# Four of a quad's seven products in one PSUM bank, and two more pairs with two quad chunks

## The chip, the cores and the metric

The kernel runs on one NeuronCore of one Trainium2 chip. The metric is the device time of one execution in microseconds; lower is better. A time is given as the median of several runs, and one further execution is recorded by the hardware profiler: its rows are what the text below reads.

## The reference, cut to what matters

One decoder layer over 256 tokens of width 2048: a mixer of three branches (differential attention, a convolution module, chunkwise retention) with gates, a cross-attention into 256 memory tokens, and a SwiGLU feed-forward network, each behind an RMS norm.

```python
proj = h @ w_in                         # 2048 -> 15360 columns
...
merged = g0 * (ya @ w_branch[0]) + g1 * (yb @ w_branch[1]) + g2 * (yr @ w_branch[2])
x = x + merged @ w_out
...
q = h @ wq; k, v = split(m @ wkv)       # cross-attention
x = x + o @ wo
...
a, b = split(h @ w13)                   # 2048 -> 2 x 5632
x = x + (silu(a) * b) @ w2              # 5632 -> 2048
```

Everything is float32, and nearly all of the work is the products with the weights, 449.63 MB of HBM reads in all.

## The kernel before

The token axis is two tiles of 128 (t = 0, 1). A weight matrix is read in chunks of 512 rows by 512 columns; a half of one (256 rows, two k-slices of 128) is a tile `raw` of 128 x 1024. Each half is split into a high part `wh` (fp32r, a cast on ScalarE, `hi_of`) and a low part `wl` (a subtract on VectorE, `lo_of`). TensorE then multiplies three times for each k-slice: activation high by weight high, high by low, low by high, each 128 x 128 by 128 x 512 columns (`products`, L293). So a half against both token tiles is 12 matmuls.

`pair` (L405) makes two blocks of 512 output columns, W0 and W1, from four activation chunks. An "N" chunk has four halves (two for each block), 48 matmuls. An "S" chunk uses seven products instead of eight (a quad, `quad_jobs`, L332), each of 6 matmuls, 42 in all. Weight tiles of such products are sums of quarters: `add` (VectorE) puts one tile onto another, and `gd(..., accum_op=ALU.add)` lets a DMA on GpSimd's queue add one from HBM. The tile t["a"] goes b11, +b12, +b22, +b21 in place and serves p1, p5, p6 and p4 in turn; t["b"] serves p7. The activation side has four combinations made once by `factors`. `MODES2` is SSNN, `MODES1` is SNNN, `MODES0` is NNNN; there are 26 pairs of this kind, in the input projection, the memory's key and value projection, the output projections, and the feed-forward network.

PSUM has eight banks. The pool `psm` holds two buffers of two banks (tiles `mm`), one for each block: ps0 and ps1, where [0] and [1] are the two token tiles. The pool `pst` has four single banks (tiles `tp`). In the kernel before, p1, p5, p6 and p7 of both S chunks are each added up in a `tp` bank of their own, and read out: join1 (a ScalarE copy of 512), join5, join6 and join7 (one, two and two VectorE steps of 512) collect them into two SBUF tiles x0 and x1. p2 and p4 go to ps0's two banks, p3 to ps1's first, on top of the N halves. `done` adds x to the finished buffer (one VectorE add of 1024 for each block) and hands it to the pair's evacuation function. The order of the code is p1, p2 and p5, p3 and p6 mixed with block 0's N halves, then p7, p4 mixed with block 1's first N halves, done for block 0, the rest of block 1, done for block 1.

The order on each engine is not the code's: the tile framework orders instructions by a simulated timeline, with waits put in where tiles and banks need them. DMAs keep the code's order on their queues. `emit_unit` prepares four units ahead (LA = 4), so a unit's cast and subtract are called for before the matmuls of the unit four places earlier. `hlp` has five buffers each for wh and wl, `rawp` ten for raw.

Of the kernel before, what the change touches and what calls it, by code (L numbers as in the profile page):

```python
# [13 lines left out]
ALU = mybir.AluOpType  # L14
# [43 lines left out]
def trunk(ctx, tc, xT, xtok, memT, memtok, w_in, w_br, w_out, w_q, w_kv, w_o, w_13, w_2,  # L58
          prm, cst, decay, gfin, out):
    nc = tc.nc  # L60
    P = 128
# [11 lines left out]
    pin = [False]  # L73
# [19 lines left out]
    def gd(**kw):  # L93
        tc.keep_in_program_order(nc.gpsimd.dma_start(**kw))  # L94
# [10 lines left out]
    def S4(shape, dt=F32):  # L105
        return s4.tile(shape, dt, tag="s4", name=nm("s4"))
# [67 lines left out]
    def call(fn):  # L174
        items.append(("call", fn))
# [117 lines left out]
    def products(u, only=None, final=True):  # L293
        a = u["act"]
        for k in range(2):
            for ps, key, k0, t, kind in u["prods"]:
                if only is not None and t not in only:
                    continue
                ah, al = lhs(a, kind, (t, k0) if kind == "n" else t, k)
                o = ps[key]  # L300
                fl = (id(ps), key)
                pe.matmul(o, ah, u["hi"][:, k, :], start=fl in u["start"] and k == 0, stop=False)
                pe.matmul(o, ah, u["lo"][:, k, :], start=False, stop=False)
                pe.matmul(o, al, u["hi"][:, k, :], start=False, stop=fl in u["stop"] and k == 1)
# [27 lines left out]
    def quad_jobs(pp, ps0, ps1, w0, w1, a):  # L332
# [62 lines left out]
        def f4(u):  # L395
            parts(u, t.pop("a"))

        return dict(p1=unit(pp, 1, 0, 0, "n", f1, b11=w0[:, 0:2, :]),
                    p2=unit(ps0, 0, 2, 0, "n", f2, b21=b21, b12=w1[:, 0:2, :]), p5=unit(pp, 5, 0, 0, "s", f5),
                    p3=unit(ps1, 0, 0, 3, "s", f3, b22=b22), p6=unit(pp, 6, 0, 1, "s", f6),  # L400
                    p7=unit(pp, 7, 0, 2, "s", f7), p4=unit(ps0, 1, 2, 1, "n", f4))

    insb = [False]

    def pair(W0, W1, acts, modes, evac0, evac1):  # L405


        ps0, ps1, pp = {}, {}, {}
        xs = []
        us = []  # L410
        sset = [c for c in range(len(acts)) if modes[c] == "S"]
        nset = [c for c in range(len(acts)) if modes[c] == "N"]

        def enter():
            settle(3)
            cap[0] = 3
            pin[0] = True

        def join1():
            x0, x1 = S4([P, 2, 512]), S4([P, 2, 512])  # L420
            xs.extend([x0, x1])
            sc.copy(x0[:, 0, :], pp.pop(1))

        def join5():
            ve.tensor_tensor(out=xs[1][:, 1, :], in0=pp.pop(5), in1=xs[0][:, 0, :], op=ALU.add)

        def join6():

            p = pp.pop(6)
            ve.tensor_tensor(out=xs[1][:, 0, :], in0=p, in1=xs[1][:, 1, :], op=ALU.subtract)  # L430
            ve.tensor_tensor(out=xs[0][:, 1, :], in0=p, in1=xs[0][:, 0, :], op=ALU.subtract)

        def join7():
            p = pp.pop(7)
            ve.tensor_tensor(out=xs[0][:, 1, :], in0=p, in1=xs[0][:, 1, :], op=ALU.subtract)
            ve.tensor_tensor(out=xs[1][:, 1, :], in0=xs[1][:, 0, :], in1=p, op=ALU.subtract)
            cap[0] = 4

        def done(n, ps, evac):
            def f():  # L440
                x = xs[n]
                ve.tensor_tensor(out=x, in0=ps["m"], in1=x, op=ALU.add)
                xs[n] = None
                insb[0] = True
                evac(x)
                insb[0] = False
            return f

        call(enter)
        quads = [quad_jobs(pp, ps0, ps1, W0[c], W1[c], acts[c]) for c in sset]  # L450
        n0, n1 = (each_half(ps, [W[c] for c in nset], [acts[c] for c in nset]) for ps, W in ((ps0, W0), (ps1, W1)))

        def units_of(*names):
            return [q[n] for m in names for q in quads for n in m]

        first = units_of(("p1",), ("p2", "p5"), ("p3", "p6"))
        marks = {len(quads) - 1: join1, 3 * len(quads) - 1: join5, 5 * len(quads) - 1: join6}

        def marked(i, f):
            def g():  # L460
                u = f()
                if i in marks:
                    call(marks[i])
                return u
            return g

        us += mixed([marked(i, f) for i, f in enumerate(first)], n0)
        us += [f() for f in units_of(("p7",))]
        call(join7)
# [1110 lines left out]
```

## Time and profile before

| what | us |
|---|---|
| median of three runs (1997.3, 2001.64, 2002.55) | 2001.64 |
| the profiled execution's own time | 1998.88 |
| its span | 1997.1 |
| PE, DVE and ACT busy | 1979.9, 1666.9, 1120.4 |

In the profile PE is TensorE, DVE VectorE, ACT ScalarE, POOL GpSimd, and SP the engine whose queue loads the weights. PEld is TensorE's weight load, which runs beside the matmuls. Nearly every instruction goes through one helper and has the line L86, so instructions are told apart by their tiles: `wh`, `wl` and `raw` as above, `mm` and `tp` the two kinds of PSUM tiles, `s` the SBUF work tiles. Matmuls are pipelined and their ends are modelled; a distance between starts is a better price than a length. A table by stretches gives the busy time of each engine in a window of the span; a row of the timeline ends with the idle time before it and who ended it.

### The profile page before, as it was taken

Reading aid. Unit: us, or ns where it says so; the run is one execution under the profiler, and the core shown is the slowest. Engines: PE = TensorE matmul, PEld = TensorE weight load, DVE = VectorE, ACT = ScalarE, POOL = GpSimd, SP = SyncE. Lnnn points to the kernel's source line nnn. Section 1 sums busy time; section 2 is a strip of 40 time slices with the busy share of each in tenths; the row PEclk is TensorE's granted clock in tenths of the full one; section 3 lists DMA queues with packets and bytes.
Section 4 is the critical chain, followed back from the end, with each engine's and each line's share of the span. In section 5 each row is a group of like instructions: output and inputs, shape, how many; then the busy total and the mean of one; then the engine's idle time right before and its main releaser. Section 6 shows DMA issues by size and latency. Waiting matters only on the chain.

```text
span 1997.1 us, 25285 instructions
## 1 busy us (share of the span) xinstructions
PE 1979.9 (99%) x9081; PEld 1636.8 (82%) x9081; DVE 1666.9 (83%) x2040; ACT 1120.4 (56%) x1343; POOL 129.8 (6%) x172
## 2 busy tenths in 40 slices
PE   9999999999999999999999999999999999999998
PEld 7888888888788887888888888888888878878886
DVE  6997689778887788989988565899988999889974
ACT  7444343548655556655566554665655665655653
POOL 0000000000100001000111000000001000011000
PEclk9999999999999999999999999999999999999999
DMA  9656555554777788689898544957888978988891
GB/s 377 206 193 197 180 177 166 180 170 151 214 208 240 235 262 257 221 263 283 274 295 304 191 158 136 287 177 224 271 274 276 275 231 252 301 278 260 256 329 61
DMA packets 128285, 463.88 MB, mean 232 GB/s; under 512 B 14368, under 2 KB 14624, under 8 KB 128160
## 3 DMA queue, kind: packets, MB, share of 16 engines
q1 hardware_dynamic: 105552, 380.46, 54.1%
q0 software_dynamic: 22464, 81.80, 19.3%
q8 instruction: 71, 1.16, 0.2%
q14 instruction: 54, 0.44, 0.1%
q10 hardware_dynamic: 144, 0.01, 0.0%
HBM read 449.63 MB, written 12.58 MB: 231 GB/s over the span
## 4 chain that ended last, share of the span: by engine, by line
PE 79%; issue 9%; DVE 6%; DMA 4%; POOL 1%; ACT 1%; SPq 0%; ACTq 0%; POOLq 0%; DVEq 0%
PE mm L86 64%; PE tp L86 15%; DVE wl L86 3%; DVE s L86 2%; DMA raw<-in_w 2%; DMA raw<-in_w_kv 1%; DMA raw<-in_w_in 1%; POOL raw L94 1%; DVE raw L86 1%; ACT wh L86 1%; DMA s<-in_memtok 0%; SPq L97 0%; POOL s L94 0%; ACTq L1575 0%; POOL x2d L94 0%
## 5 line engine op out<-in xcount | busy, mean ns | idle before, releaser
L86 PE MATMUL mm<-wh,s 128*128 128x512 f32 x4568 | 1443.9, 391 | 3.5 <-ACT wh L86 3.3
L86 ACT CAST wh<-raw 128x1024 fp32r<-128x1024 f32 (+1 forms) x855 | 886.4, 1051 | 728.7 <-PE mm L86 474.9
L86 DVE TENSOR_TENSOR wl<-raw,wh 128x1024 fp32r<-128x1024 f32 (+1 forms) x855 | 1020.8, 1217 | 252.7 <-ACT wh L86 241.3
L86 PEld LDWEIGHTS mm<-wh,s 128*128 128x128 f32 x4568 | 857.7, 188 | 183.1 <-ACT wh L86 7.0
L86 PE MATMUL mm<-wl,s 128*128 128x512 f32 x2284 | 893.2, 391 | 4.4 <-DVE wl L86 4.4
L86 PEld LDWEIGHTS mm<-wl,s 128*128 128x128 f32 x2284 | 429.5, 188 | 97.3 <-DVE wl L86 9.3
L86 PE MATMUL tp<-wh,s 128*128 128x512 f32 x864 | 288.5, 392 | 0.0
L86 PEld LDWEIGHTS tp<-wh,s 128*128 128x128 f32 x864 | 162.2, 188 | 33.1
L86 PE MATMUL tp<-wl,s 128*128 128x512 f32 x432 | 168.1, 389 | 0.0
L86 DVE TENSOR_TENSOR s<-s,s 128x1024 f32<-128x1024 f32 (+4 forms) x144 | 140.8, 986 | 1.7 <-ACT wh L86 1.1
L86 DVE TENSOR_TENSOR s<-tp,s 128x512 f32<-128x512 f32 (+1 forms) x166 | 109.6, 683 | 16.4 <-PE tp L86 11.7
L86 DVE TENSOR_TENSOR raw<-raw,raw 128x1024 f32<-128x1024 f32 x100 | 121.0, 1216 | 0.4
L86 DVE SCALAR_TENSOR_TENSOR s<-s,prm_t,s 128x256 fp32r<-128x256 f32 (+25 forms) x256 | 105.8, 461 | 0.0
L86 DVE TENSOR_TENSOR s<-mm,s 128x1024 f32<-128x1024 f32 (+1 forms) x70 | 83.1, 1187 | 20.3 <-PE mm L86 20.1
L86 PEld LDWEIGHTS tp<-wl,s 128*128 128x128 f32 x432 | 81.2, 188 | 16.2
L86 ACT ACTIVATE s<-s 128x512 f32<-128x512 f32 (+1 forms) x60 | 46.2, 771 | 63.3 <-DVE s L86 51.4
L94 POOL DMA_DIRECT2D raw<-in_w x54 | 47.7, 883 | 431.8 <-DVE wl L86 188.4
L86 PE MATMUL tp<-cst_t,s 128*128 128x128 f32 x408 | 57.1, 272 | 0.0
L86 PEld LDWEIGHTS tp<-cst_t,s 128*128 128x128 f32 x408 | 48.6, 140 | 9.0 <-issue 0.3
L86 PE MATMUL tp<-s,s 128*128 128x256 f32 (+4 forms) x348 | 53.5, 314 | 0.0
L86 PEld LDWEIGHTS tp<-s,s 128*128 128x128 f32 (+1 forms) x348 | 46.1, 189 | 5.8 <-issue 0.5
L86 ACT COPY s<-tp 128x512 f32<-128x512 f32 (+1 forms) x69 | 35.8, 528 | 15.0 <-PE tp L86 13.3
(88 smaller groups left out, 503.2 us busy)
## 6 DMA issues: line engine op xcount, KB each, us to landing
raw<-in_w SPq DMA_DIRECT2D x264, 512.0 KB, 6.5
raw<-in_w_in SPq DMA_DIRECT2D x239, 512.0 KB, 4.6
raw<-in_w_kv SPq DMA_DIRECT2D x64, 512.0 KB, 5.4
raw<-in_w POOLq DMA_DIRECT2D x54, 512.0 KB, 8.5
raw<-in_w_br SPq DMA_DIRECT2D x48, 512.0 KB, 6.5
raw<-in_w_out SPq DMA_DIRECT2D x32, 512.0 KB, 7.6
raw<-in_w_q SPq DMA_DIRECT2D x32, 512.0 KB, 5.1
raw<-in_w_o SPq DMA_DIRECT2D x32, 512.0 KB, 4.0
```

Of the source, the lines that this page charges most:

```text
L86: i = f(*a, **k)
L94: tc.keep_in_program_order(nc.gpsimd.dma_start(**kw))
```

## The change

p1, p6, p7 and p4 now share one bank, ps1[1] (in `quad_jobs`, c1 is ps1 and its key 1). The four are added up on top of each other in it; between them ScalarE copies out the running sum: keep1 after p1, keep(0) after p6, keep(1) after p7, and done1's copy at the end. Only p5 still has a `tp` bank. p2 goes to ps1[0], p3 to ps0[0]. VectorE subtracts p5's bank from two of the copies, adds block 0 (1024) in done0, and adds only half of block 1 (512) in done1. The two blocks' roles in the quad are exchanged, and the signs in `factors` follow. p6 comes before p3; f6 now does the add of b22 and starts the accumulating DMA of b21, and b22's raw tile is held from p6 to p3. The last N half of block 0 is put behind p7 instead of ahead of it. In the first pair of the key and value projection and in the feed-forward pair i = 1 MODES1 becomes MODES2.

```diff
-                pe.matmul(o, ah, u["hi"][:, k, :], start=fl in u["start"] and k == 0, stop=False)
+                sk = dict(skip_group_check=True) if ps.get("open") and key == 1 else {}
+                pe.matmul(o, ah, u["hi"][:, k, :], start=fl in u["start"] and k == 0, stop=False, **sk)
...
-        def f3(u):
-            r = raw(ix["b22"])
-            add(t["a"], r)
-            parts(u, r)
-            raws.pop(ix["b22"])
-
         def f6(u):
+            t["r"] = raw(ix["b22"])
+            add(t["a"], t["r"])
             parts(u, t["a"])
             gd(out=t["a"], in_=b21, accum_op=ALU.add)
 
+        def f3(u):
+            parts(u, t.pop("r"))
+            raws.pop(ix["b22"])
...
-        return dict(p1=unit(pp, 1, 0, 0, "n", f1, b11=w0[:, 0:2, :]),
-                    p2=unit(ps0, 0, 2, 0, "n", f2, b21=b21, b12=w1[:, 0:2, :]), p5=unit(pp, 5, 0, 0, "s", f5),
-                    p3=unit(ps1, 0, 0, 3, "s", f3, b22=b22), p6=unit(pp, 6, 0, 1, "s", f6),
-                    p7=unit(pp, 7, 0, 2, "s", f7), p4=unit(ps0, 1, 2, 1, "n", f4))
+        return dict(p1=unit(c1, 1, 0, 0, "n", f1, b11=w0[:, 0:2, :]),
+                    p2=unit(c1, 0, 2, 0, "n", f2, b21=b21, b12=w1[:, 0:2, :]), p5=unit(pp, 5, 0, 0, "s", f5),
+                    p6=unit(c1, 1, 0, 1, "s", f6, b22=b22), p3=unit(c2, 0, 0, 3, "s", f3),
+                    p7=unit(c1, 1, 0, 2, "s", f7), p4=unit(c1, 1, 2, 1, "n", f4))
...
+        def keep1():
+            xs.extend([S4([P, 2, 512]), S4([P, 2, 512])])
+            sc.copy(xs[1][:, 0, :], ps1[1])
+
+        def keep(i):
+            def f():
+                x = xs[0][:, i, :]
+                sc.copy(x, ps1[1])
+                ve.tensor_tensor(out=x, in0=pp[5], in1=x, op=ALU.subtract)
...
+        def done1():
+            x = xs[1]
+            ve.tensor_tensor(out=x[:, 0, :], in0=ps1[0], in1=x[:, 0, :], op=ALU.add)
+            sc.copy(x[:, 1, :], ps1[1])
...
+        us += mixed(units_of(("p1",), then=keep1) + units_of(("p2", "p5"))
+                    + units_of(("p6",), then=keep(0)) + units_of(("p3",)), n0[:-1])
+        us += [f() for f in units_of(("p7",), then=keep(1))]
+        us.append(n0[-1]())
+        call(done0)
         us += mixed(units_of(("p4",)), n1[:len(n1) // 2])
-        call(done(0, ps0, evac0))
         us += [f() for f in n1[len(n1) // 2:]]
-        call(done(1, ps1, evac1))
+        call(done1)
...
-            pair(w0, w1, mm, MODES2 if m or h else MODES1, ev_kv(dst[h]), ev_kv(dst[h + 1]))
+            pair(w0, w1, mm, MODES2, ev_kv(dst[h]), ev_kv(dst[h + 1]))
...
-                pair(w0, w1, x2n, MODES1 if i == 1 else MODES2, ev_a(i), ev_b(i))
+                pair(w0, w1, x2n, MODES2, ev_a(i), ev_b(i))
```

The order on TensorE shows the meeting of p7 and p4, here in the feed-forward pair i = 2. Before, p7 of the second chunk (weights wh_2326, bank tp_2335) and p4 of the first (wh_2328, in the buffer mm_2297) are woven into each other:

```order
L86 MATMUL tp_2335_11878<-wh_2324_11818,s4_2173_11121 128x512
L86 MATMUL tp_2335_11878<-wh_2326_11834,s4_2190_11208 128x512
L86 MATMUL mm_2297_11695<-wh_2328_11844,s4_2163_11075 128x512
L86 MATMUL tp_2335_11878<-wl_2327_11835,s4_2190_11208 128x512
L86 MATMUL tp_2335_11878<-wh_2326_11834,s4_2191_11209 128x512
L86 MATMUL tp_2335_11878<-wh_2326_11834,s4_2190_11208 128x512
L86 MATMUL tp_2335_11878<-wl_2327_11835,s4_2190_11208 128x512
L86 MATMUL tp_2335_11878<-wh_2326_11834,s4_2191_11209 128x512
L86 MATMUL mm_2319_11798<-wh_2331_11858,s4_2207_11294 128x512
```

Now, in the same pair, p7 of the second chunk (wh_2294) and p4 of the first (wh_2299) write the same bank of the buffer mm_2257, and all of block 0's N halves stand ahead of them:

```order
L86 MATMUL mm_2257_11635<-wh_2294_11796,s4_2160_11182 128x512
L86 MATMUL mm_2257_11635<-wl_2295_11797,s4_2160_11182 128x512
L86 MATMUL mm_2257_11635<-wh_2294_11796,s4_2161_11183 128x512
L86 MATMUL mm_2257_11635<-wh_2299_11818,s4_2133_11049 128x512
L86 MATMUL mm_2257_11635<-wl_2300_11819,s4_2133_11049 128x512
L86 MATMUL mm_2257_11635<-wh_2299_11818,s4_2134_11050 128x512
```

The two groups were in different banks and are in one now, and the block 0 half that the code puts between them has moved ahead of p7. The pairs i = 1, 5 and 6 have the same order.

At the end of the same pair ScalarE now has the copy of block 1's second half (s4_2266 from mm_2257) among the casts of weight halves; wh_2336 is for the pair that follows:

```order
L86 CAST wh_2323_11944<-raw_2321_11938 128x1024
L86 CAST wh_2325_11960<-raw_2315_11908 128x1024
L86 CAST wh_2328_11981<-raw_2327_11979 128x1024
L86 CAST wh_2336_12005<-raw_2334_11999 128x1024
L86 COPY s4_2266_11668<-mm_2257_11635 128x512
L86 CAST wh_2340_12020<-raw_2318_11920 128x1024
```

Before, VectorE alone read that buffer (mm_2319), with one add of 1024:

```order
L86 TENSOR_TENSOR wl_2354_11968<-raw_2351_11961,wh_2353_11967 128x1024
L86 TENSOR_TENSOR raw_2348_11941<-raw_2348_11941,raw_2365_12023 128x1024
L86 TENSOR_TENSOR wl_2357_11986<-raw_2355_11983,wh_2356_11985 128x1024
L86 TENSOR_TENSOR s4_2293_11687<-mm_2319_11798,s4_2293_11687 128x1024
L86 TENSOR_TENSOR wl_2359_12004<-raw_2345_11929,wh_2358_12003 128x1024
```

The copy is a new instruction on ScalarE between a cast of a weight tile and the next one; VectorE's add of that buffer is half as wide.

## Rows read from the trace of the kernel before

**Rows 1.** the page's engine line: busy us, share of the span, instructions

```profile
PE 1979.9 (99%) x9081; PEld 1636.8 (82%) x9081; DVE 1666.9 (83%) x2040; ACT 1120.4 (56%) x1343; POOL 129.8 (6%) x172
```

**Rows 2.** the chain that ended last, 1880 to 1960: start us, us, what

```profile
1909.26 21.77 PE mm L86 x96
```

**Rows 3.** groups by line and shape: busy us, mean ns, idle before, releasers

```profile
L86 DVE TENSOR_TENSOR wl<-raw,wh 128x1024 fp32r<-128x1024 f32 x853 | 1019.4, 1218 | 251.1 <-ACT wh L86 239.7 <-DMA raw<-in_w_in 5.1 <-DMA raw<-in_w_q 4.5
L86 PE MATMUL mm<-wl,s 128*128 128x512 f32 x2284 | 893.2, 391 | 4.4 <-DVE wl L86 4.4
L86 ACT CAST wh<-raw 128x1024 fp32r<-128x1024 f32 x853 | 885.2, 1052 | 727.2 <-PE mm L86 474.9 <-DMA raw<-in_w 63.0 <-PE tp L86 39.5
...
L86 DVE TENSOR_TENSOR s<-tp,s 128x512 f32<-128x512 f32 x108 | 71.7, 683 | 11.8 <-PE tp L86 11.7
...
L86 ACT COPY s<-tp 128x512 f32<-128x512 f32 x50 | 28.8, 589 | 6.0 <-PE tp L86 4.3 <-DVE s L86 1.7
```

**Rows 4.** PE's waits, 200 to 1926: us in total, times, longest

```profile
PE mm L86 <- DVE wl L86: 4.4, 7, 1.0
PE mm L86 <- ACT wh L86: 2.9, 4, 1.2
```

**Rows 5.** stretches: length, busy of PE, PEld, DVE, ACT, POOL, clock, DMA, GB/s

```profile
535.00:538.00 3.00, 1.79 (x8) 1.18 (x7) 3.00 (x11) 1.89 (x2) 0.00 (x0) 1.00 1.02 412
788.00:791.00 3.00, 1.97 (x8) 0.84 (x6) 2.68 (x6) 2.35 (x5) 1.16 (x1) 1.00 1.02 336
797.00:839.00 42.00, 42.00 (x191) 34.82 (x190) 41.35 (x52) 25.86 (x36) 1.22 (x2) 1.00 0.69 238
845.00:848.00 3.00, 2.03 (x9) 1.36 (x8) 3.00 (x3) 3.00 (x4) 0.86 (x1) 1.00 0.77 220
1336.00:1378.20 42.20, 42.20 (x192) 34.99 (x191) 39.70 (x42) 23.39 (x25) 2.60 (x3) 1.00 0.66 199
1531.00:1533.00 2.00, 1.33 (x7) 0.76 (x6) 1.80 (x3) 0.99 (x2) 0.00 (x0) 1.00 1.02 414
1617.00:1622.00 5.00, 3.98 (x17) 2.58 (x16) 4.45 (x5) 5.00 (x6) 0.00 (x0) 1.00 0.73 278
1700.00:1703.00 3.00, 2.12 (x10) 1.44 (x9) 1.30 (x2) 2.38 (x3) 0.00 (x0) 1.00 1.03 418
1782.00:1787.00 5.00, 3.57 (x15) 2.31 (x14) 3.99 (x5) 3.11 (x4) 0.00 (x0) 1.00 1.02 395
1842.90:1884.80 41.90, 41.90 (x190) 34.78 (x189) 37.40 (x37) 25.14 (x27) 3.45 (x4) 1.00 0.85 252
```

**Rows 6.** timeline, 1616: start, us, engine, line, operation, tiles, idle before

```profile
1616.46 5.80 ACT L86 CAST wh<-raw 128x1024 fp32r<-128x1024 f32 x6 [5.41 <-DMA raw<-in_w]
```

**Rows 7.** timeline, 1782 to 1787

```profile
1783.97 0.49 PE L86 MATMUL mm<-wl,s 128*128 128x512 f32 x1 [0.76 <-DVE wl L86]
...
1785.03 1.22 DVE L86 TENSOR_TENSOR wl<-raw,wh 128x1024 fp32r<-128x1024 f32 x1
...
1786.30 0.50 PE L86 MATMUL mm<-wl,s 128*128 128x512 f32 x1 [0.68 <-DVE wl L86]
```

**Rows 8.** DMA issues: KB each, median us from issue to landing

```profile
raw<-in_w POOLq DMA_DIRECT2D x54, 512.0 KB, 8.5
```

**Rows 9.** timeline at three pair ends: last matmul, then VectorE's add

```profile
1461.02 0.39 PE L86 MATMUL mm<-wh,s 128*128 128x512 f32 x1
...
1461.45 1.22 DVE L86 TENSOR_TENSOR s<-mm,s 128x1024 f32<-128x1024 f32 x1 [0.36 <-PE mm L86]
...
1629.01 0.39 PE L86 MATMUL mm<-wh,s 128*128 128x512 f32 x1
...
1632.43 1.22 DVE L86 TENSOR_TENSOR s<-mm,s 128x1024 f32<-128x1024 f32 x1
...
1880.74 0.39 PE L86 MATMUL mm<-wh,s 128*128 128x512 f32 x1
...
1883.14 1.22 DVE L86 TENSOR_TENSOR s<-mm,s 128x1024 f32<-128x1024 f32 x1
```

More of the change, by code (lines that the diff above doesn't have):

```diff
@@ L301, in products @@
                 fl = (id(ps), key)
-                pe.matmul(o, ah, u["hi"][:, k, :], start=fl in u["start"] and k == 0, stop=False)
-                pe.matmul(o, ah, u["lo"][:, k, :], start=False, stop=False)
-                pe.matmul(o, al, u["hi"][:, k, :], start=False, stop=fl in u["stop"] and k == 1)
+                sk = dict(skip_group_check=True) if ps.get("open") and key == 1 else {}
+                pe.matmul(o, ah, u["hi"][:, k, :], start=fl in u["start"] and k == 0, stop=False, **sk)
+                pe.matmul(o, ah, u["lo"][:, k, :], start=False, stop=False, **sk)
+                pe.matmul(o, al, u["hi"][:, k, :], start=False, stop=(fl in u["stop"] or "ends" in u) and k == 1, **sk)
     def emit_unit(i):
@@ L330, in block, with quad_jobs @@
         call(lambda: evac(ps["m"]))
-    def quad_jobs(pp, ps0, ps1, w0, w1, a):
+    def quad_jobs(pp, c1, c2, w0, w1, a):
         def unit(ps, key, k0, t, kind, fn, **w):
@@ L396, in f4 @@
             parts(u, t.pop("a"))
-        return dict(p1=unit(pp, 1, 0, 0, "n", f1, b11=w0[:, 0:2, :]),
-                    p2=unit(ps0, 0, 2, 0, "n", f2, b21=b21, b12=w1[:, 0:2, :]), p5=unit(pp, 5, 0, 0, "s", f5),
-                    p3=unit(ps1, 0, 0, 3, "s", f3, b22=b22), p6=unit(pp, 6, 0, 1, "s", f6),
-                    p7=unit(pp, 7, 0, 2, "s", f7), p4=unit(ps0, 1, 2, 1, "n", f4))
+        return dict(p1=unit(c1, 1, 0, 0, "n", f1, b11=w0[:, 0:2, :]),
+                    p2=unit(c1, 0, 2, 0, "n", f2, b21=b21, b12=w1[:, 0:2, :]), p5=unit(pp, 5, 0, 0, "s", f5),
+                    p6=unit(c1, 1, 0, 1, "s", f6, b22=b22), p3=unit(c2, 0, 0, 3, "s", f3),
+                    p7=unit(c1, 1, 0, 2, "s", f7), p4=unit(c1, 1, 2, 1, "n", f4))
     insb = [False]
     def pair(W0, W1, acts, modes, evac0, evac1):
-        ps0, ps1, pp = {}, {}, {}
+        ps0, ps1, pp = {}, {"open": True}, {}
         xs = []
@@ L416, in enter @@
             cap[0] = 3
[L417 to L439, printed above, removed]
-            def f():
[L441 to L446, printed above, removed]
-            return f
+        def keep1():
+            xs.extend([S4([P, 2, 512]), S4([P, 2, 512])])
+            sc.copy(xs[1][:, 0, :], ps1[1])
@@ new lines, in keep, with done0 @@
+        def keep(i):
+            def f():
+                x = xs[0][:, i, :]
+                sc.copy(x, ps1[1])
+                ve.tensor_tensor(out=x, in0=pp[5], in1=x, op=ALU.subtract)
+                if i:
+                    pp.pop(5)
+                    cap[0] = 4
+            return f
+        def done0():
+            x = xs[0]
+            ve.tensor_tensor(out=x, in0=ps0["m"], in1=x, op=ALU.add)
+            xs[0] = None
+            insb[0] = True
+            evac0(x)
+            insb[0] = False
@@ L449, in pair @@
+        def done1():
+            x = xs[1]
+            ve.tensor_tensor(out=x[:, 0, :], in0=ps1[0], in1=x[:, 0, :], op=ALU.add)
+            sc.copy(x[:, 1, :], ps1[1])
+            xs[1] = None
+            insb[0] = True
+            evac1(x)
+            insb[0] = False
         call(enter)
-        quads = [quad_jobs(pp, ps0, ps1, W0[c], W1[c], acts[c]) for c in sset]
+        quads = [quad_jobs(pp, ps1, ps0, W1[c], W0[c], acts[c]) for c in sset]
         n0, n1 = (each_half(ps, [W[c] for c in nset], [acts[c] for c in nset]) for ps, W in ((ps0, W0), (ps1, W1)))
-        def units_of(*names):
-            return [q[n] for m in names for q in quads for n in m]
@@ L456, in pair, with units_of, last @@
[L456 to L463, printed above, removed]
-                return u
[L465 to L469, printed above, removed]
+        def units_of(*names, then=None):
+            fs = [q[n] for m in names for q in quads for n in m]
+            def last():
+                u = fs[-1]()
+                u["ends"] = True
+                call(then)
+                return u
+            return fs if then is None else fs[:-1] + [last]
@@ L470, in pair @@
+        us += mixed(units_of(("p1",), then=keep1) + units_of(("p2", "p5"))
[3 more added lines that the diff above has]
+        call(done0)
         us += mixed(units_of(("p4",)), n1[:len(n1) // 2])
-        call(done(0, ps0, evac0))
         us += [f() for f in n1[len(n1) // 2:]]
-        call(done(1, ps1, evac1))
-        def unpin():
-            pin[0] = False
@@ L478, in pair @@
-        call(unpin)
+        call(done1)
         close(us)
@@ L600, in factors @@
         a11, a12, a21, a22 = (q[:, 2 * k:2 * k + 2, t * P:(t + 1) * P] for t in range(2) for k in range(2))
-        for o, x, y, op in ((0, a22, a21, ALU.subtract), (2, a11, a21, ALU.subtract),
-                            (1, a22, fv[:, 2], ALU.add), (3, a12, fv[:, 1], ALU.subtract)):
+        for o, x, y, op in ((0, a21, a22, ALU.subtract), (2, a11, a21, ALU.subtract),
+                            (1, fv[:, 0], a11, ALU.subtract), (3, a12, fv[:, 1], ALU.add)):
             ve.tensor_tensor(out=fv[:, o], in0=x, in1=y, op=op)
```

## The prediction

> **What bounds the kernel now.** I read the page's engine line first: TensorE (PE) is busy for 99% of the span, VectorE (DVE) for 83%, ScalarE (ACT) for 56% [rows 1]. So only what lengthens or shortens PE's row of matmuls counts, and DVE's hours count only where PE waits for them. Next I took the price of one 512-column matmul from the chain of waits in a stretch where nothing waits: 96 in 21.77 us, 0.2268 us each [rows 2]. The modelled length of one is 0.391 [rows 3], so a wait of PE costs 0.391 - 0.2268 = 0.164 us more than the idle time shown. The list of PE's waits between the start-up and the tail is short: 7 times for VectorE's low parts (4.4 us), 4 times for ScalarE's high parts (2.9) [rows 4]. With 11 x 0.164 that is 7.3 + 1.8 = 9.1 us in all. The table by stretches says where: in seven stretches PE is busy 1.79 of 3.00 us, 1.97 of 3, 2.03 of 3, 1.33 of 2, 3.98 of 5, 2.12 of 3 and 3.57 of 5, which is 7.2 us idle, nearly all of it [rows 5]. The timeline shows the pattern of most of them: a cast on ScalarE stands for 5.41 us on a weight tile [rows 6], and behind it come a cast, a subtract and PE (0.76 us idle at 1783.97, 0.68 at 1786.30) [rows 7]. That tile is the one that f6's accumulating DMA on GpSimd's queue fills for p4; such a DMA takes 8.5 us to land [rows 8]. The stretch at 845 is another thing: DVE is busy for all 3.00 us there, so it is behind. The granted clock is 1.00 in all of these, stalls or not [rows 5].
>
> **Fewer matmuls.** In two pairs a second chunk goes from eight half products to seven: 48 - 42 = 6 matmuls each, 12 x 0.2268 = **-2.7 us**. Those two pairs pay on DVE: three more low parts and two more adds of weights, 5 x 1.218 = +6.1 us each [rows 3]. Both already have a full VectorE: 41.35 us of 42.00 in the key and value pair, 39.70 of 42.20 in the FFN pair [rows 5]. With 6.1 more and the 2.6 of the next paragraph less, 44.9 and 43.2 us of work meet matmuls of 40.6 and 40.8. VectorE falls some 4 and 2.4 us behind, in stretches in which it also makes the factors of later chunks, which can slip into the next pair. Bounds: 0 (all of it slips, as now, where PE is busy 42.00 of 42.00 beside the full VectorE) and +6 (PE waits for all of it). The row is near the first end: I take **+1**.
>
> **DVE and ACT.** Each of the 26 pairs gives up the work of four 512-wide VectorE steps (join5, join6 and join7 had five and the two dones a 1024 each; the keeps have two, done0 a 1024 and done1 a 512, so five 512s and two 1024s become three and one), in the built programs -52 x 0.683 and, with the two pairs' new work, -16 x 1.218: -55 us of 1667. ScalarE takes 78 copies of 512 more at 0.589, +46, and 6 casts at 1.05, in all +52 us on 1120 [rows 1, 3]. Per FFN pair DVE goes from 37.40 in 41.9 us to about 34.9 [rows 5]. Both lie beside PE and are worth 0 by themselves.
>
> **The old stalls.** p6 now comes ahead of p3, and the last half of block 0 and p7 behind it, so from f6's DMA to p4's cast there are 18 matmuls more, 18 x 0.2268 = 4.1 us. The worst of these waits of ScalarE was 5.41 us, and it cost PE 5.00 - 3.98 + 2 x 0.164 = 1.35 us [rows 5, 6]. With 4.1 us more lead PE should not see any of them. Without the stretch at 845 (0.97 + 0.16) the waits are worth 9.1 - 1.1 = 8.0. Bounds: -9 (845 goes too, since DVE has less to do) and 0 (the DMA is issued 4.1 us earlier, lands among SP's loads and is as late as before: the same 8.5 us DMA queues behind the same loads). I take **-7**.
>
> **The new waits.** p1, p6, p7 and p4 follow each other in one bank, with ScalarE reading it out between them. Three prices come from the timeline: a reader starts 0.43 us after the start of the matmul that it waits for (matmul 1461.02, DVE 1461.45) [rows 9]; the copy of 512 takes 0.589 [rows 3]; PE starts 0.05 after the end of what it waits for (1785.03 + 1.22, PE at 1786.30) [rows 7]. From one matmul's start to the next dependent one's that is 0.43 + 0.59 + 0.05 = 1.07 us, where 0.23 would be the pitch: **0.84 us** for each place where no other work stands between. The order of the built program shows which places: in four FFN pairs the block 0 half that the code puts behind p7 was moved ahead of it, so p4's first matmul stands right behind p7's last in the same bank; 4 x 0.84 = 3.4, and one pair of the first stage has a single matmul between them, +0.6. **+4.0**. In the other 21 pairs an N unit of 12 matmuls (2.72 us) covers the 0.84, and the copy between p6 and p7 is covered by p3 everywhere.
>
> The Trainium skill ("PSUM — Partial Sum Buffer", its summary of rules) says that PSUM is to be read from another bank than the one the matmuls are running into, and guarded by bank. By that rule the wait costs its 0.84 at those five places and cannot be shortened by reading the first columns early; without it, it would be 0 there and the sum 4 us lower. The trace agrees for the other-bank case: at 1461.45 VectorE reads a finished buffer while PE goes on at the pitch.
>
> **The end of a pair.** done1 was one VectorE add; now block 1's second half leaves by a ScalarE copy too. Its place in ScalarE's order is behind the cast for the next pair's p1, which waits for a buffer that the first p1 unit of that pair releases. The count from the last matmul of the pair: six matmuls (1.36), then 0.20 to ScalarE's start, cast 1.05, copy 0.59, PE 0.05, 3.25 us. In ten boundaries PE comes back to that buffer after two p1 units, 12 x 0.2268 = 2.72: it waits 0.53, **+5.3 us** in all. In seven others there are 18 matmuls (4.1) and nothing is seen; the rest have more. Bounds: 0 (the cast is let go early) and +10 (below). ScalarE does keep its order when it waits: for 5.41 us nothing else runs on it [rows 6].
>
> **Smaller places**: the last pair of the output projection, whose end comes with VectorE behind, and one pair with p2 right behind p1's copy: **+1.3** (0 to +4).
>
> **Sum.** -2.7 + 1 - 7 + 4.0 + 5.3 + 1.3 = +1.9 us. On the profiled run (1998.88 us, of which the span is 1997.1) that gives 2000.8; that run lies 2.8 below the median of the runs shown, 2001.64, on which it gives 2003.5. I say **2002**.
>
> **Rivals.** What can be told from no change is 0.3%, 6 us either way.
> - *The relief wins* (0.22). All of the old stalls go, 845 with them (-9), and the new waits are smaller: the cast ahead of done1's copy comes free earlier than I count, since PE's slack is eaten by whichever wait comes first, and two waits in a row overlap. For it: with DVE at 35 of 42 us every low part is early. Against: the 0.84 is a straight chain in one bank. -2.7 - 9 + 4 + 1 = -7 from the median: 1995.
> - *DVE is late at a pair's end* (0.22), the slower side. The add of done1 now guards half of a buffer and the copy the other half, and the next user needs both. At two ends before, the add started at 1632.43 and 1883.14 though the last matmuls had started at 1629.01 and 1880.74: 3.4 and 2.4 us where 0.43 would do, 3.0 and 2.0 late; at 1461.45 it was on time [rows 9]. It decides from 1.2 us on: then VectorE, not the copy, is last, and PE waits for (lateness - 1.2) on top of the 0.53. PE did not wait at those ends, as nothing came back so early. If the relief does not reach that instruction (it stands behind low parts that wait for casts, and those wait for the accumulating DMA), the ten ends cost 0.5 to 1.8 each, 10 instead of 5.3, and the old stalls stay at -2: -2.7 + 3 (the second S chunks) - 2 + 4 + 10 = +12, 2014.
> - *The cover is too thin*, the half of it that is left does not do what it says: keep(1)'s copy stands two casts back in ScalarE's order, which has 52 us more to do. Then 0.84 + 2 x 1.05 = 2.94 meets the 2.72 of the N unit, 21 x 0.22 = +5 on the forecast, 2007. ScalarE at 59% speaks against two casts late at once; I count it within the slower case.
>
> **Chances and range.** Forecast 0.56, relief 0.22, late ends 0.22. Faster by over 0.3% takes the relief case, slower the third, the rest is within 0.3%. The bounds of the unknown terms (-9 to 0, 0 to +10, 0 to +4, 0 to +6), on the median with -2.7 + 4.0, reach from 1994 to 2023, and to 1990 if the five places of 4.0 are covered too; both ends need all at once, so the range is 1992 to 2011; the likeliest case alone has 1997 to 2007.
>
> **What would show it.** In the profile after: PE's waits for ScalarE's copies on the mm tile, some 0.6 to 0.7 us idle at four or five places right behind p7, and about ten of 0.4 or less at pair ends; the seven stretches of [rows 5] at full PE, apart from 845; casts with waits for raw tiles of under 2 us; DVE's sum near 1612 us, ACT's near 1173, 12 matmuls fewer. It is wrong if PE's idle time on copies is above 12 us or below 4, or if waits for p4's low parts remain.

## The result, and the profile after

The changed kernel is slower: 2023.24 us, the median of 6 runs (2021.81 to 2028.67), against 2000.73 (6 runs) for the kernel before; ratio 1.012, 95% interval 1.0105 to 1.0135. The forecast was 2002 with a range of 1992 to 2011. The profiled execution took 2028.67 us, its span is 2026.5; it is the highest of the six. A second profile of the same kernel (e9 below) has a span of 2019.5 and waits at the same places, three of them of other sizes, so I read places from the first and the sum from both.

The page's engine line after:

```profile
PE 1990.3 (98%) x9069; PEld 1639.5 (81%) x9069; DVE 1635.4 (81%) x1972; ACT 1168.2 (58%) x1427; POOL 133.2 (7%) x176
```

Against [rows 1], 12 matmuls are gone and ScalarE has 48 us more, near the 52 forecast. VectorE lost 31.5 us of busy time, not 55. Added up one by one, the lengths of its steps fell by 49 us; but steps that follow each other overlap (before, from 1632.43 to 1633.57 for one of 1.22 us, a pitch of 1.14), which a product of counts and lengths leaves out, and with more idle time fewer follow each other.

PE's waits between 200 and 1950 (in total, times, longest):

```profile
PE mm L86 <- ACT s L86: 13.1, 20, 2.5
PE mm L86 <- DVE wl L86: 6.3, 4, 2.9
PE tp L86 <- DVE s L86: 3.9, 2, 3.7
PE tp L86 <- DVE wl L86: 0.8, 1, 0.8
PE mm L86 <- ACT wh L86: 0.3, 1, 0.3
```

They answer to [rows 4]: 24.4 us in 28 waits, with 0.164 each 29.0, where there were 9.1. Half is for a kind of wait that was not there before: the copies of the shared bank (`s`) on ScalarE. The waits for casts (`wh`) are nearly gone. The table by stretches, columns as in [rows 5]:

```profile
792.00:795.00 3.00, 0.82 (x2) 0.72 (x3) 1.13 (x4) 2.68 (x7) 0.86 (x2) 0.89 1.02 415
841.00:844.00 3.00, 1.07 (x5) 0.78 (x5) 3.00 (x4) 3.00 (x5) 0.00 (x0) 1.00 0.97 180
847.00:851.00 4.00, 0.50 (x1) 0.50 (x2) 4.00 (x6) 2.50 (x4) 0.00 (x0) 0.74 0.49 165
1355.00:1365.00 10.00, 6.15 (x27) 4.18 (x26) 10.00 (x10) 5.04 (x7) 0.86 (x1) 0.97 0.56 138
1384.00:1387.00 3.00, 2.33 (x11) 1.60 (x10) 2.85 (x4) 2.31 (x3) 0.00 (x0) 1.00 0.90 295
1554.00:1557.00 3.00, 1.76 (x9) 1.12 (x8) 1.58 (x2) 2.65 (x4) 0.00 (x0) 1.00 1.03 421
1808.00:1813.00 5.00, 2.46 (x9) 1.68 (x8) 3.54 (x5) 3.17 (x5) 0.00 (x0) 0.85 1.03 416
```

In the two pairs that became MODES2 (841 to 851 and 1355 to 1365) VectorE is busy for all of the time and PE is not. At 792, 1554 and 1808 VectorE has time to spare and DMA is full. At 1384 only 0.68 is lost.

Three timelines show the three kinds of wait on a copy. The bare meeting of p7 and p4, with no other matmul between, in the feed-forward pair i = 1:

```profile
1384.65 0.39 PE L86 MATMUL mm<-wh,s 128*128 128x512 f32 x1
1385.08 0.59 ACT L86 COPY s<-mm 128x512 f32<-128x512 f32 x1 [0.30 <-PE mm L86]
...
1385.72 0.50 PE L86 MATMUL mm<-wh,s 128*128 128x512 f32 x1 [0.68 <-ACT s L86]
```

1385.72 - 1384.65 = 1.07 us, 0.84 over the pitch, the number forecast. It stands at four places (1386, 1429, 1640, 1683). Then the end of a pair:

```profile
1399.98 2.14 ACT L86 CAST wh<-raw 128x1024 fp32r<-128x1024 f32 x2 [1.95 <-PE mm L86]
...
1401.95 0.39 PE L86 MATMUL mm<-wh,s 128*128 128x512 f32 x1
1402.02 0.57 ACT L86 COPY s<-mm 128x512 f32<-128x512 f32 x1
...
1402.64 0.50 PE L86 MATMUL mm<-wh,s 128*128 128x512 f32 x1 [0.31 <-ACT s L86]
```

done1's copy comes behind two casts, the first of which waited 1.95 us for PE; PE loses 0.31 + 0.16 = 0.47 (forecast 0.53), at nine ends, and 0.53 + 0.16 at a tenth. And this, the longest of three, in the second pair of the second output group of the feed-forward network:

```profile
1806.07 0.39 PE L86 MATMUL mm<-wh,s 128*128 128x512 f32 x1
1806.08 2.00 ACT L86 CAST wh<-raw 128x1024 fp32r<-128x1024 f32 x2 [3.06 <-DMA raw<-in_w]
...
1808.57 0.39 PE L86 MATMUL mm<-wh,s 128*128 128x512 f32 x1
1809.91 1.04 ACT L86 CAST wh<-raw 128x1024 fp32r<-128x1024 f32 x1 [1.83 <-DMA raw<-in_w]
1810.86 0.58 ACT L86 COPY s<-mm 128x512 f32<-128x512 f32 x1
...
1811.49 0.80 PE L86 MATMUL mm<-wh,s 128*128 128x512 f32 x1 [2.54 <-ACT s L86]
```

The two waits are for p4's two weight tiles, which f6's accumulating DMAs fill. The copy behind them is keep(1). p7's last matmul started at 1806.07, so by the 0.43 us of [rows 9] the bank could have been read from 1806.50 on, and the copy comes 4.36 us later than that. Block 0's N half covers the first part of it, until its last matmul at 1808.57. The first p4 weights have been cast by then, but PE goes on only at 1811.49, after 2.54 us of idle time. GpSimd's queue shows when the DMAs were started:

```profile
1786.99 0.56 POOL L94 DMA_DIRECT2D x2d<-s  x1 [8.52 <-DVE s L86]
1787.54 1.10 POOL L94 DMA_DIRECT2D s<-x2d  x2
1788.60 0.96 POOL L94 DMA_DIRECT2D raw<-in_w  x1
1790.06 0.87 POOL L94 DMA_DIRECT2D raw<-in_w  x1 [0.50 <-issue]
1792.80 0.87 POOL L94 DMA_DIRECT2D raw<-in_w  x1 [1.86 <-DVE wl L86]
```

The queue stands for 8.52 us until VectorE has made what the first transfer takes; then six transfers are started in 6 us, and the one of 1792.80 is not there before the cast of 1809.91, 17 us later, where 8.5 is the median [rows 8]. It is not this queue alone that is slow. The loads that SyncE starts in the same stretch (1790 to 1800) are as late, 13.2 us where their median over the program is 6.2, and the DMA engines are full (1.03 in the row of 1808):

```profile
raw<-in_w SPq DMA_DIRECT2D x5, 512.0 KB, 13.2
raw<-in_w POOLq DMA_DIRECT2D x2, 512.0 KB, 16.5
```

So the DMA lands late in a stretch in which the other loads do so too; how much of its lateness comes from the queue's own wait before it, no run separates.

By cause, each wait with its 0.164, in the first profile after: the two MODES2 pairs 1.93 + 3.75 + 0.83 + 2.88 + 0.66 = 10.0; copies held up on ScalarE (794, 1556, 1811) 2.28 + 1.24 + 2.54 + 0.49 = 6.6; four bare meetings 3.4; ten pair ends 5.0; three other copies 1.6; waits of the old kind at 521, 522 and 771 2.3. That is 28.9; 9.1 are gone, and 2.7 for the 12 matmuls. So 17.1 us come from waits. To it come matmuls at half clock behind long waits: in the first profile 30 of them at 0.427 us, 6.0 us, in the second 6, 1.2 us. With 0.8 to 2.0 us at the start of the program and 2 to 3 us in distances a little over the pitch, each too short for the list of waits and of unknown cause, this is about the 22.4 (span 2019.5) and most of the 29.4 (2026.5) over the span before.

### The profile page after: what moved, and what is told of

It reads as the page before. It is cut to its first block, busy times and chain, and to the rows that moved or that the text cites. A ratio compares the mean times of both kernels' runs of the same rounds, so it can differ in the third digit from the quotient of the medians.

```text
span 2026.5 us, 25239 instructions
## 1 busy us (share of the span) xinstructions
PE 1990.3 (98%) x9069; PEld 1639.5 (81%) x9069; DVE 1635.4 (81%) x1972; ACT 1168.2 (58%) x1427; POOL 133.2 (7%) x176
## 4 chain that ended last, share of the span: by engine, by line
PE 88%; DVE 4%; DMA 3%; issue 3%; ACT 2%; POOL 0%; SPq 0%; ACTq 0%; POOLq 0%; DVEq 0%
PE mm L86 79%; PE tp L86 9%; DVE s L86 2%; DMA raw<-in_w 2%; DVE wl L86 2%; ACT wh L86 1%; DMA raw<-in_w_out 1%; ACT s L86 1%; DMA s<-in_memtok 0%; DVE raw L86 0%; DMA raw<-in_w_in 0%; SPq L97 0%; POOL raw L94 0%; ACT L86 0%; ACTq L1572 0%
## 5 line engine op out<-in xcount | busy, mean ns | idle before, releaser
L86 PE MATMUL mm<-wh,s 128*128 128x512 f32 x5152 | 1620.4, 392 | 14.9 <-ACT s L86 13.1
L86 PEld LDWEIGHTS mm<-wh,s 128*128 128x128 f32 x5152 | 969.8, 188 | 226.5 <-ACT s L86 22.1
L86 PE MATMUL mm<-wl,s 128*128 128x512 f32 x2576 | 1008.5, 392 | 7.4 <-DVE wl L86 7.3
L86 PEld LDWEIGHTS mm<-wl,s 128*128 128x128 f32 x2576 | 485.4, 188 | 109.5 <-DVE wl L86 10.4
L86 PE MATMUL tp<-wh,s 128*128 128x512 f32 x272 | 93.2, 401 | 3.7 <-DVE s L86 3.7
L86 DVE TENSOR_TENSOR s<-tp,s 128x512 fp32r<-128x512 f32 (+1 forms) x114 | 75.8, 684 | 8.9 <-ACT s L86 4.2
L86 ACT COPY s<-mm 128x512 f32<-128x512 f32 x104 | 60.5, 586 | 18.0 <-PE mm L86 17.4
L86 PEld LDWEIGHTS tp<-wh,s 128*128 128x128 f32 x272 | 52.2, 192 | 14.6 <-DVE s L86 4.0
L86 PE MATMUL tp<-wl,s 128*128 128x512 f32 x136 | 54.1, 398 | 0.8 <-DVE wl L86 0.8
L86 ACT CAST s<-tp 128x512 fp32r<-128x512 f32 x58 | 31.3, 587 | 10.1 <-PE tp L86 10.0
```

What stands on the lines that cost most here:

```text
L86: i = f(*a, **k)
```

## The experiments

All were timed in 5 rounds beside the kernel before, whose median was 2000.4 us in the first four, 2000.71 in the next four and 2001.82 in the last four.

**e1, MODES1 again in both pairs.**

```diff
-            pair(w0, w1, mm, MODES2, ev_kv(dst[h]), ev_kv(dst[h + 1]))
+            pair(w0, w1, mm, MODES2 if m or h else MODES1, ev_kv(dst[h]), ev_kv(dst[h + 1]))
...
-                pair(w0, w1, x2n, MODES2, ev_a(i), ev_b(i))
+                pair(w0, w1, x2n, MODES1 if i == 1 else MODES2, ev_a(i), ev_b(i))
```

> The changed kernel with MODES1 (one quad chunk) in the two pairs where it had become MODES2; the shared bank stays. Theory A (the second quad chunk overfills VectorE in those two pairs): in the changed kernel PE is idle 1.93 us at 843, 3.75 at 851, 0.83 at 1360 and 2.88 at 1364 and then runs 17 matmuls at 0.427 us, 9.4 + 4 x 0.16 + 17 x 0.2 = 13.4 us, against 12 matmuls saved, 2.7; so this run is 10.7 us below the changed kernel, about 2012.5, with these four waits gone. Theory B (the shared bank with its copies makes all of the loss): the 12 matmuls come back and nothing goes, 2026. Theory C (both): between, the rest in waits for copies.

2015.33 us, ratio 1.0077 (1.0065 to 1.0089): 8 us below the changed kernel, nearer to A than to B, but not all of it. The four waits are gone; two new ones for copies came in the same pairs (1.49 at 838, 2.56 at 1369). So the shared bank with its order costs 15 us without any more quad chunks (no run has the shared bank with the old order of p3 and p6). The wait at 1369 is that of keep(0) behind two casts:

```profile
1365.99 1.04 ACT L86 CAST wh<-raw 128x1024 fp32r<-128x1024 f32 x1 [1.66 <-PE mm L86]
1366.95 1.04 ACT L86 CAST s<-s 128x1024 fp32r<-128x1024 f32 x1
1367.89 0.58 ACT L86 COPY s<-mm 128x512 f32<-128x512 f32 x1
...
1368.52 0.50 PE L86 MATMUL mm<-wh,s 128*128 128x512 f32 x1 [2.56 <-ACT s L86]
```

The cast ahead of the copies waits, for its buffer, until the last matmul before p7 has started (the 1.66): so keep(0) cannot be done in time, however early p6 was.

**e2, the kernel before with MODES2 in both pairs.**

```diff
-            pair(w0, w1, mm, MODES2 if m or h else MODES1, ev_kv(dst[h]), ev_kv(dst[h + 1]))
+            pair(w0, w1, mm, MODES2, ev_kv(dst[h]), ev_kv(dst[h + 1]))
...
-                pair(w0, w1, x2n, MODES1 if i == 1 else MODES2, ev_a(i), ev_b(i))
+                pair(w0, w1, x2n, MODES2, ev_a(i), ev_b(i))
```

> The kernel before with MODES2 in the same two pairs and nothing else; its own banks and joins. Theory A: VectorE, with 2.6 us a pair more to do than in the changed kernel, falls behind at least as far, 10 to 14 us above the kernel before, 2011 to 2015, with waits of PE for VectorE near 845 and 1360. Theory B: 12 matmuls fewer and no copies, -2.7 to 0, 1998 to 2001.

2015.14 us, ratio 1.0074 (1.0062 to 1.0086), 15 us above the kernel before: A, without any shared bank. VectorE falls behind until PE, already in the next pair, stands for 7 us for the adds that end the feed-forward pair (the timeline there):

```profile
1391.28 2.35 DVE L86 TENSOR_TENSOR wl<-raw,wh 128x1024 fp32r<-128x1024 f32 x2
1393.55 1.22 DVE L86 TENSOR_TENSOR raw<-raw,raw 128x1024 f32<-128x1024 f32 x1
1394.69 2.35 DVE L86 TENSOR_TENSOR s<-mm,s 128x1024 f32<-128x1024 f32 x2
...
1396.05 0.77 PE L86 MATMUL mm<-wh,s 128*128 128x512 f32 x1 [7.01 <-DVE s L86]
```

**e3, MODES1 again in the key and value pair only** (the first of e1's two lines).

> The changed kernel with MODES1 in the first key and value pair only; the feed-forward pair i = 1 keeps MODES2. Theory A: the waits at 843 and 851 with the 11 matmuls at 0.427 us go, 5.7 + 0.3 + 2.2 - 1.4 = 6.8 us below the changed kernel, 2016.5, and those at 1360 to 1364 stay. Theory B: +1.4, 2024.6.

2015.58 us, ratio 1.0083 (1.007 to 1.0096), A's number within 1 us. With e1 it says that the key and value pair's second chunk costs 7 to 8 us and the feed-forward pair's about nothing on top of e1: there it trades the waits at 1360 and 1364 for the one at 1369 and six matmuls.

**e4, TensorE's order from p7 to p4 kept as in the code.**

```diff
-PIN = ()
+PIN = ("pe",)
...
+        call(lambda: pin.__setitem__(0, True))
         us += [f() for f in units_of(("p7",), then=keep(1))]
         us.append(n0[-1]())
         call(done0)
         us += mixed(units_of(("p4",)), n1[:len(n1) // 2])
+        call(lambda: pin.__setitem__(0, False))
```

> The changed kernel with TensorE's order from p7 to p4 kept as in the code, so that block 0's last N half stands between p7 and p4 in every pair. If a copy out of the shared bank costs PE 0.84 us wherever nothing stands between: the four waits of 0.68 us at 1386, 1429, 1640 and 1683 go, 4 x 0.84 = 3.4 us below the changed kernel, 2019.8. If the wait only moves to the next unit (p4's low part or its DMA): less than 1 us, 2022.5 to 2023.5.

2034.29 us, ratio 1.0174 (1.0161 to 1.0187): 11 us above the changed kernel, which neither expectation has. The four waits of 0.68 are gone, but the order that was kept holds the small transposes of the side tasks too, and they now stand in PE's way until VectorE has made their input. PE's waits:

```profile
PE tp L86 <- DVE s L86: 13.6, 4, 4.7
PE mm L86 <- ACT s L86: 10.6, 17, 3.0
```

As a test of the cover it is spoilt; what it shows is that the scheduler's freedom to move those transposes is worth more than the cover.

**e5, the kernel before with p6 ahead of p3.**

```diff
-        def f3(u):
-            r = raw(ix["b22"])
-            add(t["a"], r)
-            parts(u, r)
-            raws.pop(ix["b22"])
-
         def f6(u):
+            t["r"] = raw(ix["b22"])
+            add(t["a"], t["r"])
             parts(u, t["a"])
             gd(out=t["a"], in_=b21, accum_op=ALU.add)
+
+        def f3(u):
+            parts(u, t.pop("r"))
+            raws.pop(ix["b22"])
...
-        first = units_of(("p1",), ("p2", "p5"), ("p3", "p6"))
-        marks = {len(quads) - 1: join1, 3 * len(quads) - 1: join5, 5 * len(quads) - 1: join6}
+        first = units_of(("p1",), ("p2", "p5"), ("p6",), ("p3",))
+        marks = {len(quads) - 1: join1, 3 * len(quads) - 1: join5, 4 * len(quads) - 1: join6}
```

> The kernel before with one thing of the change: p6 ahead of p3, so that f6 adds b22 and starts the accumulating DMA of b21 three matmul groups earlier; own banks, joins and MODES1 as before. Theory A (the old stalls at 536, 789, 1532, 1618, 1700, 1783 and 1785 are that DMA coming late for p4): they go, 6 to 8 us below the kernel before, 1992.5 to 1994.5. Theory B (the DMA lands late whenever it is started, or the waits move to the next weight tile): within 2 us of it, 1998.5 to 2002.5.

1998.44 us, ratio 0.9988 (0.998 to 0.9997): 2.3 us below, between the two. The waits at 536 and from 1532 to 1786 are all gone, as A has it. Those at 791 (2.04 and 0.44) and 844 (1.48 and 0.45) have grown; the first stands behind ScalarE's work on a memory token tile (e12), the second is where VectorE was behind before. PE's waits:

```profile
PE mm L86 <- ACT wh L86: 4.4, 4, 2.0
PE mm L86 <- DVE wl L86: 0.2, 1, 0.2
PE tp L86 <- DVE wl L86: 0.2, 1, 0.2
```

**e6, e1 with done1's copy on VectorE.**

```diff
-            sc.copy(x[:, 1, :], ps1[1])
+            ve.tensor_copy(x[:, 1, :], ps1[1])
```

> The kernel of e1 (shared bank, MODES1) with done1's copy on VectorE instead of ScalarE. Theory A (the copy is late because it stands behind a cast on ScalarE): the ten waits of 0.31 us at pair ends go, 10 x 0.47 = 4.7 us below e1, 2010.6; the waits for the copies between p6 and p4 stay. Theory B (VectorE is behind at a pair's end, add and copy come after its backlog): 0 to 8 us above e1, 2015 to 2023, with waits of PE for VectorE's s tiles at pair ends.

2022.12 us, ratio 1.0112 (1.0097 to 1.0128), 7 above e1. B's number, but not by the wait that B names: the waits of 0.31 for the copy turn into waits of 0.37 for the low part that VectorE makes next, and two copies that stand behind casts are later, 2.71 and 2.32 us of idle PE against 1.46 and 0.71. The profiled run, 2017.95, is the lowest of the four, 3.5 above e1's profiled run; the rest of the 7 is not in it.

```profile
1390.45 0.68 DVE L86 COPY s<-mm 128x512 f32<-128x512 f32 x1
...
1391.05 1.22 DVE L86 TENSOR_TENSOR wl<-raw,wh 128x1024 fp32r<-128x1024 f32 x1
...
1392.32 0.50 PE L86 MATMUL mm<-wl,s 128*128 128x512 f32 x1 [0.37 <-DVE wl L86]
```

**e7, e1 with all four copies on VectorE** (the same edit in keep1, keep and done1).

> The kernel of e1 with all four copies out of the shared bank on VectorE. Theory A (the copies wait behind casts on ScalarE that themselves wait for a DMA or for VectorE: 792, 838, 1368, 1545 and 1799 in e1, 9.6 us, and 4.7 us at pair ends): 13 to 14 us below e1 less 0.1 us at each bare meeting, 2001 to 2003. Theory B (VectorE's own order is no better, it runs up to 3 us behind): waits of PE for VectorE's copies at p4 and p7 in many pairs, 2012 to 2030.

2046.94 us, ratio 1.0233 (1.0219 to 1.0247): B's side and B's waits, but 17 us beyond its range. PE's waits:

```profile
PE mm L86 <- DVE s L86: 21.7, 21, 4.1
PE mm L86 <- ACT wh L86: 8.1, 3, 3.7
PE mm L86 <- DVE wl L86: 5.8, 13, 1.0
```

**e8, low parts of the second quad chunk on ScalarE in the two MODES2 pairs.**

```diff
-            lo_of(u, src)
+            if alt:
+                sc.copy(u["lo"], src)
+            else:
+                lo_of(u, src)
```

> The changed kernel; in the two pairs that had become MODES2 the low parts of the second quad chunk's weights are plain copies on ScalarE instead of subtracts on VectorE, so those products are computed with wrong low parts: seven steps of 1.22 us off VectorE and seven of 1.05 onto ScalarE in each of the two pairs. Theory A (VectorE is overfull there): the waits at 843, 851, 1360 and 1364 shrink by at least 8 of their 10 us and the slow matmuls behind them go, 9 to 13 us below the changed kernel, 2010 to 2014. Theory B (the banks or ScalarE hold PE there): 2022 to 2030.

2013.4 us, ratio 1.0064 (1.0051 to 1.0078), about 10 below the changed kernel: A's number, but the waits shrink by less than A asks. Those of the two pairs go from 9.4 to 4.1 us of idle (0.79 and 1.90 at 842 and 847, 0.17 and 1.25 at 1353 and 1358), by 5.3 and not by 8; the 1.90 is now for a copy on ScalarE. The rest is elsewhere: one of the copies that wait for p4's DMA was late by 0.29 instead of 1.24, one bare meeting is gone, and there were 14 slow matmuls instead of 30.

**e9, the changed kernel again** (no edit).

> The changed kernel unaltered, as the base for the run beside it: 2022 to 2025 again, with the waits of PE for ScalarE's copies at 794, 1556 and 1811 and those for VectorE at 843, 851, 1360 and 1364 at the same places if they belong to the program's order, elsewhere if they are chance.

2022.96 us, ratio 1.0109 (1.0095 to 1.0123). All of the waits are there again, to 0.03 us at the bare meetings and pair ends, 1.92, 3.73, 0.83 and 2.88 in the MODES2 pairs, and 2.51, 2.63 and 1.11 where a copy waits for a DMA (2.28, 1.24 and 2.54 in the first profile). So the places belong to the program's order, and the sizes of the last three to the DMA.

**e10, the changed kernel without the add of b21.**

```diff
             parts(u, t["a"])
-            gd(out=t["a"], in_=b21, accum_op=ALU.add)
```

> The changed kernel without f6's accumulating DMA: p4's weight tile is not given b21, so p4 multiplies a wrong sum, and one DMA in two on GpSimd's queue is gone. Theory A (keep(1)'s copy stands on ScalarE behind the cast of p4's second tile, which waits for that DMA): the waits of 1.24 at 1556 and 2.54 at 1811 and the slow matmuls behind the second go, 1.4 + 2.7 + 1.2 = 5 us below the changed kernel, 2018; the bare 0.68s and 0.31s stay. Theory B (the copy is late for another reason): these two stay, within 1.5 us of it.

2012.85 us, ratio 1.0059 (1.0046 to 1.0073): 10 us below e9, beside which it ran, twice what A has. A for the two waits: at 1556 and 1811 PE waits no more. A third, 794, is gone too; there the copy stood behind ScalarE's work on a memory token tile, whose load is on the same GpSimd queue. In e9 the three are worth 6.7 us; the rest of the 10 is in part one bare meeting that is gone (0.84) and smaller waits in the first stages, and has no test of its own. At the place of 1806.07 the copy now starts 0.42 us behind its matmul, and the N half covers it:

```profile
1794.30 0.39 PE L86 MATMUL mm<-wh,s 128*128 128x512 f32 x1
...
1794.72 0.59 ACT L86 COPY s<-mm 128x512 f32<-128x512 f32 x1 [0.53 <-PE mm L86]
```

PE's waits for copies are down to:

```profile
PE mm L86 <- ACT s L86: 9.0, 16, 3.5
```

The 3.5 stands at 844, in the full key and value pair, at the place of the 3.75 of the changed kernel. There VectorE's factor ended last, 0.26 us behind a copy; here the copy does. Both stand behind VectorE's late sum of weights.

**e11, e1 with two N halves behind p7.**

```diff
-                    + units_of(("p6",), then=keep(0)) + units_of(("p3",)), n0[:-1])
+                    + units_of(("p6",), then=keep(0)) + units_of(("p3",)), n0[:-2])
...
-        us.append(n0[-1]())
+        us += [f() for f in n0[-2:]]
```

> The kernel of e1 (shared bank, MODES1) with the last two N halves of block 0 behind p7 instead of one, so that 5.2 us of matmuls instead of 2.5 stand between p7 and p4 in 19 of the 26 pairs; four FFN pairs still have none in the built order. Theory A (keep(1)'s copy up to 4 us late behind a waiting cast): the waits at 1545 and 1799 go, 2.5 us below e1, 2013, and no wait is added. Theory B (the N halves moved behind p7 are themselves late, or the room does not matter): 2015 to 2018.

2019.06 us, ratio 1.0092 (1.0078 to 1.0106), 4 above e1. The waits at 1545 and 1799 are gone, as A has it, but PE waits for low parts 13 times instead of twice, and 10 slow matmuls came behind the wait at 1367:

```profile
PE mm L86 <- ACT s L86: 11.1, 18, 2.6
PE mm L86 <- DVE wl L86: 6.7, 13, 1.5
```

**e12, e5 with the memory tokens' squares asked for two steps later.**

```diff
             eng(out=r, in_=src[n])
             yield
+            for _ in range(2 if eng is gd else 0):
+                yield
             sumsq(r, parts[:, n, :])
```

> The kernel of e5 (before, with p6 ahead of p3) with the squares of each memory token tile asked for two steps later after its load, so that ScalarE no longer stands on that load. If ScalarE's order is what makes PE wait at 791 in e5 (2.04 + 0.44 us idle): that goes, 2.8 us below e5, 1995.6, below the kernel before by some 5. If the wait moves on to what needs the token statistics, or VectorE's backlog at 844 grows: 1998 to 2001.

1995.87 us, ratio 0.9973 (0.9963 to 0.9983), 6 below the kernel before: faster than both kernels, with the four separate banks. The wait at 791 goes from 2.04 and 0.44 to 0.16 and 0.45, nearly as forecast. But the time comes back behind it, 1.34 at 839 and 0.55 at 846, and the profiled runs of e5 and e12 are alike (1995.43 and 1995.45). e5's is one of its fastest, e12's an ordinary one. So the 2.6 us between the medians are not explained by the waits shown; that e5's other runs have a granted clock of 0.996 to 0.998 would fit slow matmuls behind its wait of 2.04, but no such run was profiled.

## Why the prediction was wrong

- **The second quad chunk, forecast +1 with 0 to +6: the first step that failed.** The profile has 10.0 us of waits there, over the upper bound. The arithmetic was right (44.9 us of VectorE work against 40.6 of matmuls, 43.2 against 40.8), and I then let all of it slip because the row of before shows a full VectorE beside a PE that never waits. Full at 41.35 of 42.00 is not over full: what is over has to be late, and what VectorE made late was not only factors but the low parts and casts behind them. e2 shows it without the bank (+15 us), e3 where (the key and value pair, 7 us), e8 that it hangs in good part on VectorE's load (5.3 of the 9.4 us of idle time there go when seven steps in each pair move to ScalarE). The 4 and 2.4 us of excess that I worked out are near the two longest waits (3.75 and 2.88); that VectorE is late at several units one after another, I had not counted.
- **The old stalls, forecast -7: the second step that failed.** As far as it says that the accumulating DMA reaches PE no longer through p4's casts, it held: [rows 5] has those stretches, and after it there is one wait for a cast (0.3). e5 tests the step by itself, and the stretches go, for 2.3 us, since the time comes back at 791 and 844. What failed is the sentence that PE should not see any of these waits. The DMA is still late twice in the feed-forward network, and ScalarE still stands for it 3.06 and 1.83 us; before, only p4's own weights were behind that wait, and PE had other work. Now keep(1) is behind it, and p4's first chunk needs keep(1). With the memory tokens' load that is 6.6 us, and the waits of the old kind are 2.3, so the term is about 0 instead of -7. e10 shows the chain by taking the DMA away; no run moves the copy ahead of the waiting cast. I had read from [rows 6] that ScalarE runs nothing else while it waits, and used it for the ends of pairs only. The Trainium skill ("PSUM — Partial Sum Buffer", its section on engine and sequencer instructions) says the same, that ScalarE's and VectorE's queues are strictly first in, first out; the trace agrees, with nothing on ScalarE in those 3.06 and 1.83 us.
- **The bare meetings, +4.0:** four at 0.84, 3.4 us, and small ones. Right to 0.01 us each. The rule that I had weighed from the Trainium skill ("PSUM — Partial Sum Buffer", its summary of rules), to read PSUM from another bank than the one that matmuls run into, agrees with it: PE waited at each such place.
- **The pair ends, +5.3:** 5.0. Right, and for the reason given.
- **The smaller places, +1.3:** 1.6.
- **The matmuls, -2.7:** right.
- **The clock was not in the sum.** Each of the four waits of 2.3 to 3.8 us was followed by 6 to 11 matmuls at 0.427 us in the first profile, one of four in the second: 6.0 and 1.2 us. Before, no wait was that long.
- **The sum again.** From the +1.9 forecast to the 22.4 of the second profile: 9.0 for the second chunk, about 7 for the old stalls and the copies that took their place, -0.6 for the other three terms together, 1.2 of slow matmuls, 0.8 at the start, and 2 to 3 in the short distances. With one quad chunk in both pairs, the same terms without the second chunk gave +3.6, where e1 measured +15: so the second chunk is less than half of the loss, and copies held up on ScalarE are its other main part (9.6 us in e1, at 792, 838, 1369, 1545 and 1799).
- **The rivals.** The slower case had the right side and too small a size, by another mechanism: VectorE's add is not late at the ends of the feed-forward pairs after the change. PE's idle time on copies, 13.1 us, is over the 12 that I had named as the mark of a wrong forecast. "The cover is too thin" came nearest for the second step: keep(1) is late where N units cover it, not by two casts in 21 pairs but by a DMA in two.

The relief of VectorE, 2.6 us in a pair, shows nowhere in PE's waits. Before, the stretch at 845 was the one of [rows 5] where VectorE itself was behind, and there the change gave it more work than it took away. No run tests the relief by itself.

## What to carry to other kernels

A read of an accumulator that the next matmul needs should not stand in an in-order engine behind work that waits for a transfer: then lateness that was hidden on that engine can reach TensorE, as far as no other matmuls cover it. Before counting a saved buffer or a shorter chain, list what stands ahead of each new link in its engine's order and what that waits for. And compare the work of a stage with its length: here VectorE at 98% of a stage cost nothing, and at some 111% and 106% it cost 6.0 and 4.0 us, where the excess was 4 and 2.4.

## What the runs showed of the hardware that was not expected

The clock behind a wait is not the same in each run of one program. In the first profile of the changed kernel PE stands for 3.75 us until 850.50, and the next 11 matmuls take 0.427 us each; the granted clock of that stretch is 0.52, the lower of its two levels (1.2 of 2.4 GHz). In the second profile PE stands for 3.73 us at the same place, and goes on at the full clock. The two rows, first of the first, then of the second profile (columns as in [rows 5]):

```profile
851.00:856.00 5.00, 5.00 (x13) 3.83 (x13) 4.74 (x6) 1.05 (x1) 0.86 (x1) 0.52 0.21 16
```

```profile
849.30:853.00 3.70, 3.68 (x16) 3.07 (x17) 3.70 (x5) 1.64 (x2) 0.57 (x1) 1.00 0.00 0
```

13 matmuls in 5.00 us, against 16 in 3.70. Of the 7.0 us between the two profiles' spans, 4.8 are such slow matmuls (30 against 6, 0.2 us each). That a kernel with long waits scatters more from run to run is not shown: the six runs of the changed kernel lie within 6.9 us, the six of before within 5.3, but fifteen of before, beside e5 to e8, within 7.7.
